# Projection units beside HGRN as eight plain products, their low parts on DVE

## The chip, the cores and the metric

The kernel runs on one core of one Trainium2 chip. The metric is the device time of one execution in microseconds (us), the median of several runs. The engines are named as the profile names them: PE (matrix products, with PEld for its weight loads), DVE (vector), ACT (activation), POOL (the general-purpose engine, called `gpsimd` in the code) and SP, whose queue issues the DMAs.

## The reference, cut to what matters

Two layers of a hybrid encoder over 1024 tokens of width 1024. Each layer is

```python
h = rms_norm(x, norm_g[l])
proj = einsum("bsd,de->bse", h, w_in[l])       # one combined input projection
# proj is split into xm, om, zm | hq, ff, fb, hi, hz | aq, ak, av, az
y_m = mLSTM(xm, om, zm)        # 4 heads
y_h = HGRN2(hq, ff, fb, hi, hz)  # 6 heads of 128, both directions
y_a = differential_attention(aq, ak, av, az)   # 4 heads
x = x + concat(y_m, y_h, y_a) @ w_out[l]
```

HGRN2 in one direction is the recurrence `S_t = diag(f_t) S_{t-1} + (1 - f_t) i_t^T`, `o_t = S_t^T q_t`, with `f = lb + (1 - lb) * sigmoid(ff)`. The kernel computes it for both directions at once by doubling: at level `lv` pairs of blocks of `2**lv` tokens are joined.

## The kernel before, in words

**The projection.** `w_in` is cut into 32 units of two blocks of 128 columns each; three of them (`xm`) are done at the start of a layer, 29 are a stream (`stream`, L471) that fills PE beside the other work. The normed input, transposed, is held as four operands B11, B12, B21, B22 (halves of the depth by halves of the tokens) of 128x512 pieces. Products are made in fp32r, with each fp32 factor split into a high part `whi` (an ACT copy, L163) and a low part `wlo` (what the copy left over, a subtraction on POOL, L164), and three matmuls (hi·hi, hi·lo, lo·hi) for each of four pieces of depth: twelve matmuls of 128x512 make one product (`steps12`). A unit (`unit`, from L208) is a 2x2 block product by Strassen's method in Winograd's form: seven products instead of eight, 84 matmuls, paid with four sums of weights (`wsum`, L171; `ws` in the trace) and with the sums of B (`Bt`, t1 to t4), which are made once a layer. The results go through SBUF tiles `p`, `u`, `c` to DRAM (`pr_d`).

**The order.** `fill(n)` takes the next n steps of the stream; one step is one matmul, and a few steps only issue splits. From the mLSTM heads until 48 steps after the last HGRN head, every PE instruction is tied to the one before it (`in_order`), so the order on PE there is the written one. On the other engines, and on PE in the stages behind HGRN, a scheduler orders the instructions when the kernel is built. The table `H_FILL` (L80) says how many steps stand ahead of each piece of a HGRN head.

**A HGRN head** (`hgrn`, from L854): load and transpose the values (`hvt`); tanh of the gates on ACT, from it the keys `ks` (L877, DVE) and the gates T (L879, ACT); `kd` and `qp` by `dtt` (a `scalar_tensor_tensor` of DVE, recorded at L121); the products `dg` on PE; then seven levels. At a level ACT copies the wanted halves of both directions of `ks` to `kt` (L908, levels 0 to 4), PE makes the scores `lv`, DVE merges them into `sd` under a mask (L894), multiplies `ks` and `qp` by the gates (L121, each direction by itself from level 1 on) and then T by itself (L121). After the levels come the transposes `kst`, the states `sb`/`sf` (chains `Sb`, `Sf` on DVE, L984 and L996), the output `ho`, its squares (`jk`, L1018), the normalisation `rstd` (L427 to L433), the scaling (L1024, ACT) and the transposes `hyT`. The loop over heads (L1037) runs the start of the next head ahead of the end of the current one, so that `rstd` stands behind the next head's `ks`, `kd` and `qp` on DVE.

While the heads run, `sums["pool"]` is set, and the weight sums are made on POOL too (L175).

## Time and profile before

| what | value |
|---|---|
| median of 3 runs | 3116.47 us (3112.49 to 3120.48) |
| the profiled execution | 3109.8 us, span 3108.1 us |
| PE busy | 2729.3 us, 88% of the span |
| DVE busy | 2057.1 us, 66% |
| ACT busy | 1374.4 us, 44% |
| POOL busy | 984.5 us, 32% |
| HGRN with the 48 steps behind it, layer 1 | 491 to 975 us of the span |
| the same, layer 2 | 2027 to 2511 us |
| mean granted PE clock | 0.951 |

A row of the grouped view gives the line, the engine, the operation, its operands by the program's names, the shape and the count, then the busy time and the mean duration of one, and then how long the engine stood idle just before these instructions and what ended most of that. A row of the timeline gives start and duration in us. A row of a tile view gives the shortest, the median and the longest duration in ns.

### The profile page before, as it was taken

Reading aid. Unit: us, or ns where it says so; the run is one execution under the profiler, and the core shown is the slowest. Engines: PE = TensorE matmul, PEld = TensorE weight load, DVE = VectorE, ACT = ScalarE, POOL = GpSimd, SP = SyncE. Lnnn points to the kernel's source line nnn. Section 1 sums busy time; section 2 is a strip of 40 time slices with the busy share of each in tenths; the row PEclk is TensorE's granted clock in tenths of the full one; section 3 lists DMA queues with packets and bytes.
Section 4 is the critical chain, followed back from the end, with each engine's and each line's share of the span. In section 5 each row is a group of like instructions: output and inputs, shape, how many; then the busy total and the mean of one; then the engine's idle time right before and its main releaser. Section 6 shows DMA issues by size and latency. Waiting matters only on the chain. (4 is left out here: it accounts for less than half of the span.)

```text
span 3108.1 us, 44781 instructions
## 1 busy us (share of the span) xinstructions
PE 2729.3 (88%) x16428; PEld 2243.4 (72%) x16428; DVE 2057.1 (66%) x3690; ACT 1374.4 (44%) x2832; POOL 984.5 (32%) x725
## 2 busy tenths in 40 slices
PE   6889999888889997998979999988888898879987
PEld 4777877666667776787858787876666676768875
DVE  7776546776773646997587644467766656489964
ACT  5334544434444435654153354543444444465533
POOL 4243224443433440010241432244443343301012
PEclk9899999998999998999998999999999999999998
DMA  3343333222224654420223343332222156542221
GB/s 108 109 133 120 123 125 109 96 89 89 89 79 156 214 170 117 159 81 29 82 75 116 117 131 133 99 113 93 99 92 89 65 196 219 183 134 90 67 71 72
DMA packets 186524, 351.98 MB, mean 113 GB/s; under 512 B 17968, under 2 KB 67632, under 8 KB 186304
## 3 DMA queue, kind: packets, MB, share of 16 engines
q1 hardware_dynamic: 186304, 349.12, 34.2%
q8 instruction: 129, 2.11, 0.3%
q14 instruction: 91, 0.75, 0.1%
HBM read 234.69 MB, written 114.36 MB: 112 GB/s over the span
## 5 line engine op out<-in xcount | busy, mean ns | idle before, releaser
L164 POOL TENSOR_TENSOR wlo<-wraw,whi 128x512 fp32r<-128x512 f32 x262 | 390.3, 1496 | 1292.0 <-ACT whi L163 1152.5
L164 POOL TENSOR_TENSOR wlo<-ws,whi 128x512 fp32r<-128x512 f32 x232 | 347.3, 1498 | 581.2 <-ACT whi L163 510.9
L109 PE MATMUL op<-whi,yb 128*128 128x512 f32 x1024 | 340.3, 401 | 0.6 <-DVE ayo L1181 0.4
L163 ACT ACTIVATE whi<-wraw 128x512 fp32r<-128x512 f32 x262 | 163.5, 627 | 319.1 <-issue 99.9
L163 ACT ACTIVATE whi<-ws 128x512 fp32r<-128x512 f32 x232 | 146.1, 630 | 328.2 <-PE ua L111 139.6
L111 PE MATMUL ua<-Bt,whi 128*128 128x512 f32 x742 | 269.5, 435 | 0.5 <-DVE c L252 0.3
L1271 DVE TENSOR_TENSOR xo<-op,xo 128x512 f32<-128x512 f32 x256 | 174.1, 687 | 88.8 <-PE op L109 88.0
L109 PEld LDWEIGHTS op<-whi,yb 128*128 128x128 f32 x1024 | 193.8, 190 | 44.8 <-DVE ayo L1181 1.2
L109 PE MATMUL ua<-Bt,whi 128*128 128x512 f32 x650 | 211.9, 406 | 13.7 <-ACT u L238 9.3
L109 PE MATMUL op<-wlo,yb 128*128 128x512 f32 x512 | 202.8, 396 | 0.0
L1205 ACT ACTIVATE e<-S,mx 128x1024 f32<-128x1024 f32 x128 | 142.1, 1112 | 101.9 <-DVE mx L1202 59.1
L111 PEld LDWEIGHTS ua<-Bt,whi 128*128 128x128 f32 x742 | 148.2, 203 | 34.7 <-issue 3.3
L121 DVE SCALAR_TENSOR_TENSOR qp<-qp,T 128x512 f32<-128x512 f32 (+1 forms) x156 | 166.9, 1106 | 3.6 <-PE lv L111 3.6
L121 DVE SCALAR_TENSOR_TENSOR ks<-ks,T 128x512 f32<-128x512 f32 (+1 forms) x156 | 151.6, 1001 | 23.1 <-ACT kt L908 13.8
L1201 DVE TENSOR_REDUCE mx<-S 128x1 f32<-128x1024 f32 x128 | 155.1, 1217 | 14.7 <-PE S L109 14.2
L111 PE MATMUL ua<-Bt,wlo 128*128 128x512 f32 x372 | 160.2, 431 | 0.0
L109 PE MATMUL po<-av,wT 128*128 128x128 f32 x1024 | 141.3, 285 | 20.4 <-ACT wT L1221 10.5
L109 PEld LDWEIGHTS po<-av,wT 128*128 128x128 f32 x1024 | 131.9, 197 | 33.3 <-ACT wT L1221 15.7
L109 PEld LDWEIGHTS ua<-Bt,whi 128*128 128x128 f32 x650 | 123.5, 193 | 44.4 <-ACT u L238 10.2
L908 ACT ACTIVATE kt<-ks 128x1024 f32<-128x1024 f32 x60 | 71.3, 1188 | 149.2 <-PE lv L111 57.9
L109 PE MATMUL S<-qkh 128*128 128x512 f32 x256 | 110.6, 432 | 23.1 <-ACT e L1205 22.9
L109 PE MATMUL ua<-Bt,wlo 128*128 128x512 f32 x324 | 129.9, 401 | 0.0
(433 smaller groups left out, 6749.2 us busy)
## 6 DMA issues: line engine op xcount, KB each, us to landing
wraw<-w_in SPq DMA_DIRECT2D x256, 256.0 KB
wraw<-yT SPq DMA_DIRECT2D x64, 256.0 KB
wraw<-w_out SPq DMA_DIRECT2D x64, 256.0 KB
xac<-xcd SPq DMA_DIRECT2D x16, 512.0 KB
W<-mu SPq DMA_DIRECT2D x32, 256.0 KB
xcd<-xc SPq DMA_DIRECT2D x12, 512.0 KB
xct<-tka SPq DMA_DIRECT2D x12, 512.0 KB
vd<-tkv SPq DMA_DIRECT2D x12, 512.0 KB
```

The lines of the kernel that those rows point to most:

```text
L109: return fn(*a, **k)
L111: seq["last"] = fn(*a, **k)
L121: nc.vector.scalar_tensor_tensor(out_, a, 1.0, b, op0=ALU.mult, op1=op)
L163: nc.scalar.activation(hi, src, AF.Copy)
L164: (lo_eng or nc.gpsimd).tensor_tensor(lo, src, hi.bitcast(F32), op=ALU.subtract)
L908: nc.scalar.activation(raw(kt, 0, [[2 * hs, nb], [hs, 2], [1, hs]]), raw(ks, 0, [[2 * hs, nb], [hs + S, 2], [1, hs]]), AF.Copy)
L1201: nc.vector.tensor_reduce(mx, ps, axis=AX.X, op=ALU.max)
L1205: nc.scalar.activation(e, ps, AF.Exp, scale=QK ** -0.5, bias=mx, accum_out=ls_)
L1271: nc.vector.tensor_tensor(xv, ps, xv, op=ALU.add)
```

## The change: what it does

While the HGRN heads run (`plain["on"]`), a unit is done by `unit_plain`: eight products, 96 matmuls, from B11, B21, B22 and t1 alone, where t1 is B12 - B11. For each of the two blocks: A1·B11 is copied out as `p` and stays in PSUM, where A2·B21 is added to it; A1·t1 and A2·B22 are summed in a second PSUM tile, to which `p` is added. There are no sums of weights. A unit splits four weights instead of seven, and the low part is a `tensor_tensor` on DVE instead of POOL. `H_FILL` has 16 more steps a head. In HGRN itself, T's scaling goes from ACT to DVE (a `tensor_scalar`), the `scalar_tensor_tensor` of `kd`, `qp` and the levels become `tensor_tensor`, and at every level one instruction multiplies both directions of `ks`, and one both of `qp`, through a three-dimensional pattern that goes to and fro between the two directions.

```diff
-H_FILL = {"hvt": 0, "ty": 32, "dg": 10, 0: 14, 1: 14, 2: 10, 3: 10, 4: 10, 5: 8, 6: 14, "kst": 10, "sb": 8, "ho": 10, "tail": 60}
+H_FILL = {"hvt": 0, "ty": 36, "dg": 12, 0: 14, 1: 14, 2: 12, 3: 12, 4: 12, 5: 10, 6: 14, "kst": 10, "sb": 8, "ho": 12, "tail": 60}
...
-    def split(src, lo_eng=None):
+    plain = {"on": False}
+
+    def split(src):
...
-        (lo_eng or nc.gpsimd).tensor_tensor(lo, src, hi.bitcast(F32), op=ALU.subtract)
+        (nc.vector if plain["on"] else nc.gpsimd).tensor_tensor(lo, src, hi.bitcast(F32), op=ALU.subtract)
...
     def wsum(o, a, b, op):
-        if sums["pool"]:
-            nc.gpsimd.tensor_tensor(o, a, b, op=op)
-        else:
-            dtt(o, a, b, op)
+        dtt(o, a, b, op)
...
+    def unit_plain(l, u, B, dst):
...
+        raws = [w_quad(l, u, q) for q in range(4)]
+        o1, o2 = split(raws[0]), split(raws[1])
+        yield
+        for xy in range(2):
+            psa = ps_pj(f"va{l}_{u}{xy}")
+            yield from steps12(psa, o1, B["11"], True, True)
+            p1 = tmp(f"p{xy}")
+            nc.scalar.activation(p1, psa, AF.Copy)
+            yield
+            psd = ps_pj(f"vd{l}_{u}{xy}")
+            yield from steps12(psd, o1, B["t1"], True, False)
+            if xy == 0:
+                n1 = split(raws[2])
+            yield
+            yield from steps12(psd, o2, B["22"], False, True)
+            c = tmp(f"c{xy}2")
+            nc.vector.tensor_tensor(c, psd, p1, op=ALU.add)
...
+            if xy == 0:
+                n2 = split(raws[3])
+            yield
+            yield from steps12(psa, o2, B["21"], False, True)
+            c = tmp(f"c{xy}1")
+            nc.scalar.activation(c, psa, AF.Copy)
...
-                yield from unit(l, U_OF[a, b], B, (dst_of(a), dst_of(b)))
+                yield from (unit_plain if plain["on"] else unit)(l, U_OF[a, b], B, (dst_of(a), dst_of(b)))
...
-                nc.scalar.activation(th, th, AF.Identity, scale=lb_a1[:, l, d, hd:hd + 1], bias=lb_a2[:, l, d, hd:hd + 1])
+                nc.vector.tensor_scalar(th, th, lb_a1[:, l, d, hd:hd + 1], lb_a2[:, l, d, hd:hd + 1],
+                                        op0=ALU.mult, op1=ALU.add)
...
-            dtt(kd, ks[:, 0], ks[:, 1], ALU.add)
-            dtt(qp[:, 0], T0[:, 0], q, ALU.mult)
-            dtt(qp[:, 1], T0[:, 1], q, ALU.mult)
+            nc.vector.tensor_tensor(kd, ks[:, 0], ks[:, 1], op=ALU.add)
+            nc.vector.tensor_tensor(qp[:, 0], T0[:, 0], q, op=ALU.mult)
+            nc.vector.tensor_tensor(qp[:, 1], T0[:, 1], q, op=ALU.mult)
...
-                for src, t_ in ((ks, (W + 1, 0)), (qp, (1, W))):
-                    if lv == 0:
-                        sv = raw(src, 0, [[2, nb], [1 + S, 2]])
-                        dtt(sv, sv, raw(T, t_[0], [[2, nb], [t_[1] - t_[0], 2]]), ALU.mult)
-                    else:
-                        for w in range(2):
-                            sv = raw(src, w * (hs + S), [[2 * hs, nb], [1, hs]])
-                            dtt(sv, sv, raw(T, t_[w], [[2, nb], [0, hs]]), ALU.mult)
+                el = [[2 * hs, nb], [hs + S, 2], [1, hs]]
+                tq = raw(T, 1, [[2, nb], [W - 1, 2], [0, hs]])
+                tk = raw(T, W + 1, [[2, nb], [-W - 1, 2], [0, hs]])
+                qv = raw(qp, 0, el)
+                kv = raw(ks, 0, el)
+                nc.vector.tensor_tensor(kv, kv, tk, op=ALU.mult)
+                nc.vector.tensor_tensor(qv, qv, tq, op=ALU.mult)
...
-                dtt(raw(base, 0, [[W // 2, 2], [1, W // 2]]), a0, a1, ALU.mult)
+                nc.vector.tensor_tensor(raw(base, 0, [[W // 2, 2], [1, W // 2]]), a0, a1, op=ALU.mult)
...
-        sums["pool"] = True
+        plain["on"] = True
...
-        sums["pool"] = False
+        plain["on"] = False
```

How the order of the instructions moves, at the three places that the prediction speaks of. Rows give line, operation, output and inputs, shape and count; in the kernel after, L985 and L986 are the products of `ks` and `qp`, L990 is T's, L927 the merge, L225 a unit's sum and L166 a low part.

DVE in the second head of layer 1, around levels 1 and 2, before:

```order
L894 COPY_PREDICATED sd_4991<-lvl_96,lv_5101 128x512
L121 SCALAR_TENSOR_TENSOR qp_4863<-qp_4863,T_10_5031 128x256x2 x2
L121 SCALAR_TENSOR_TENSOR ks_4864<-ks_4864,T_01_4862 128x128x4 x2
L121 SCALAR_TENSOR_TENSOR T_10_5031<-T_01_4862 128x256
L894 COPY_PREDICATED sd_4991<-lvl_97,lv_5143 128x512
L121 SCALAR_TENSOR_TENSOR qp_4863<-qp_4863,T_01_4862 128x128x4 x2
```

The same place now:

```order
L927 COPY_PREDICATED sd_4936<-lvl_96,lv_5054 128x512
L986 TENSOR_TENSOR qp_4827<-qp_4827,T_10_4986 128x256x2x2
L985 TENSOR_TENSOR ks_4828<-ks_4828,T_01_4826 128x128x2x4
L990 TENSOR_TENSOR T_10_4986<-T_01_4826 128x256
L166 TENSOR_TENSOR wlo_5393<-wraw_5254,whi_5392 128x512
L927 COPY_PREDICATED sd_4936<-lvl_97,lv_5093 128x512
L986 TENSOR_TENSOR qp_4827<-qp_4827,T_01_4826 128x128x2x4
```

Each pair of `ks` or `qp` products has become one instruction of twice the elements, in the same order, and a unit's low part stands between them.

DVE at the change of heads, from the end of head 1's state chain to its `rstd`, before:

```order
L996 SCALAR_TENSOR_TENSOR ks_4864<-ks_4864,Tc_5350,sf_5429 128x128 x4
L877 TENSOR_SCALAR ks_5504<-T_02_5502,nlb_a_114,lb_a_112 128x1024 x2
L121 SCALAR_TENSOR_TENSOR kd_5612<-ks_5504 128x1024
L121 SCALAR_TENSOR_TENSOR qp_5503<-T_02_5502,hq_5505 128x1024 x2
L252 TENSOR_TENSOR c_15_5574<-ua_15_5312,p_15_5555 128x512
L427 TENSOR_SCALAR rs_5525<-hss_5445 128x8
```

The same place now:

```order
L1028 SCALAR_TENSOR_TENSOR ks_4828<-ks_4828,Tc_5292,sf_5356 128x128 x4
L166 TENSOR_TENSOR wlo_5635<-wraw_5624,whi_5634 128x512
L909 TENSOR_SCALAR ks_5428<-T_02_5426,nlb_a_114,lb_a_112 128x1024 x2
L911 TENSOR_SCALAR T_02_5426<-T_02_5426,lb_a_112,lb_a_113 128x1024 x2
L914 TENSOR_TENSOR kd_5540<-ks_5428 128x1024
L225 TENSOR_TENSOR c_15_5475<-vd_150_5332,p_15_5330 128x512
L916 TENSOR_TENSOR qp_5427<-T_02_5426,hq_5429 128x1024
L915 TENSOR_TENSOR qp_5427<-T_02_5426,hq_5429 128x1024
L459 TENSOR_SCALAR rs_5449<-hss_5372 128x8
```

Two `tensor_scalar` (L911, T's scaling) have come in ahead of `kd`, and a low part ahead of `ks`.

POOL at the end of the mLSTM stage of layer 1 and into HGRN, before (`ws` is a sum of weights):

```order
L164 TENSOR_TENSOR wlo_4199<-ws_3932,whi_4198 128x512
L175 TENSOR_TENSOR ws_4375<-wraw_4269,wraw_4273 128x512
L164 TENSOR_TENSOR wlo_4236<-wraw_3842,whi_4235 128x512
L164 TENSOR_TENSOR wlo_4278<-wraw_4269,whi_4277 128x512
L164 TENSOR_TENSOR wlo_4282<-wraw_4271,whi_4281 128x512
```

The same place now, with the running numbers in the names (`wlo149` is the 149th):

```order
L166 TENSOR_TENSOR wlo148_4097<-ws147_4094,whi148_4096 128x512
L166 TENSOR_TENSOR wlo149_4199<-ws144_3932,whi149_4198 128x512
L166 TENSOR_TENSOR wlo243_7972<-wraw239_7963,whi243_7971 128x512
L166 TENSOR_TENSOR wlo244_7976<-wraw240_7965,whi244_7975 128x512
L166 TENSOR_TENSOR wlo247_8166<-ws246_8163,whi247_8165 128x512
```

POOL goes from the last low part ahead of HGRN (149) straight to the first behind it (243). On PE the order of the HGRN pieces is the same; the matmuls of units between them are 96 more in each layer's HGRN (1033 instead of 937 from the first `hvt` to the first `soT` behind HGRN), and 36 more from there to the end of the layer's stream (753 instead of 717).

More of the change, by code (lines that the diff above doesn't have):

```diff
@@ L169, in w_quad @@
         return load_raw(w_in[l, :, o:o + 512])
-    sums = {"pool": False}
     def wsum(o, a, b, op):
-        if sums["pool"]:
-            nc.gpsimd.tensor_tensor(o, a, b, op=op)
-        else:
-            dtt(o, a, b, op)
+        dtt(o, a, b, op)
     def w_tmp():
@@ L206, in unit_std, with tmp @@
                 evac(xy, ps, half)
+    def unit_plain(l, u, B, dst):
+        def tmp(nm):
+            return un.tile([P, 512], F32, tag="ut", name=f"{nm}{l}_{u}")
+        raws = [w_quad(l, u, q) for q in range(4)]
[15 more added lines that the diff above has]
+            nc.vector.tensor_tensor(c, psd, p1, op=ALU.add)
+            for rows, ap in dst[xy]:
+                nc.sync.dma_start(ap[:, 512:], c[rows])
+            if xy == 0:
[4 more added lines that the diff above has]
+            nc.scalar.activation(c, psa, AF.Copy)
+            for rows, ap in dst[xy]:
+                nc.sync.dma_start(ap[:, :512], c[rows])
+            if xy == 0:
+                o1, o2 = n1, n2
+                yield
     def unit(l, u, B, dst):
```

## The prediction

> **What bounds the kernel now.** The page comes first, for the engines' shares:
>
> ```profile
> span 3108.1 us, 44781 instructions
> PE 2729.3 (88%) x16428; PEld 2243.4 (72%) x16428; DVE 2057.1 (66%) x3690; ACT 1374.4 (44%) x2832; POOL 984.5 (32%) x725
> ```
>
> PE is the busiest, but 88% is a mean over stages. The change touches HGRN and, through what is left of the stream, the stage behind it. So the second view is the stages: HGRN with its 48 last steps in both layers, then the stage behind it.
>
> ```profile
> core 0: us, PE busy (x) PEld busy (x) DVE busy (x) ACT busy (x) POOL busy (x), PEclk, DMA share, GB/s
> 491.00:975.00 484.00, 400.56 (x3363) 322.79 (x3361) 335.55 (x505) 198.84 (x392) 207.57 (x125) 0.93 0.29 96
> 2027.00:2511.00 484.00, 404.03 (x3378) 326.14 (x3377) 333.05 (x508) 201.58 (x395) 209.28 (x125) 0.93 0.29 99
> 975.00:1160.00 185.00, 169.15 (x740) 136.14 (x741) 97.61 (x152) 79.16 (x165) 76.49 (x54) 0.95 0.61 201
> ```
>
> HGRN takes 484 us in either layer; PE is idle for 83 and 80 of them, 82 on average, and its clock is at 0.93. Third, the PE groups of 491 to 975, for the waits; the last three rows are of layer 2's stretch.
>
> ```profile
> L111 PE MATMUL lv<-qp,kt 128*64 128x64 f32 x960 | 38.1, 234 | 22.7 <-DVE qp L121 19.6 <-ACT u L238 1.9 <-ACT p L222 1.3
> L111 PE MATMUL kst<-ident,ks 128*128 128x128 f32 x96 | 14.0, 292 | 10.8 <-ACT kst L972 10.2 <-DVE ks L121 0.5
> L111 PE MATMUL hyT<-ident,ho 128*128 128x128 f32 x48 | 13.7, 454 | 24.4 <-ACT ho L1024 24.4
> L111 PE MATMUL ho<-hv,sc 128*128 128x128 f32 x96 | 12.3, 281 | 10.0 <-DVE Sb L984 10.0
> L111 PE MATMUL lv<-qp,ks 128*64 128x64 f32 x192 | 7.7, 240 | 6.6 <-DVE qp L121 6.6
> L111 PE MATMUL dg<-hq,kd 128*64 128x64 f32 x192 | 7.4, 233 | 3.0 <-DVE kd L121 3.0
> L111 PE MATMUL lv<-qp,ks 128*32 128x32 f32 x384 | 4.6, 199 | 5.0 <-DVE qp L121 5.0
> ...
> L111 PE MATMUL lv<-qp,kt 128*64 128x64 f32 x960 | 39.8, 240 | 25.7 <-DVE qp L121 25.6
> L111 PE MATMUL hyT<-ident,ho 128*128 128x128 f32 x48 | 13.7, 436 | 24.4 <-ACT ho L1024 24.4
> L111 PE MATMUL kst<-ident,ks 128*128 128x128 f32 x96 | 13.2, 281 | 3.7 <-ACT kst L972 3.7
> ```
>
> The waits end at DVE: the levels wait for `qp`, and `hyT` for ACT's scaling, which follows DVE's `rstd`. The units' own matmuls show hardly a wait. Why DVE is late, its groups and POOL's of the same stretch tell:
>
> ```profile
> L121 DVE SCALAR_TENSOR_TENSOR qp<-qp,T 128x512 f32<-128x512 f32 x72 | 68.4, 989 | 1.3 <-PE lv L111 1.3
> L121 DVE SCALAR_TENSOR_TENSOR ks<-ks,T 128x512 f32<-128x512 f32 x72 | 63.2, 909 | 4.5 <-PE lv L111 4.3
> L894 DVE COPY_PREDICATED sd<-lvl,lv 128x512 f32<-128x512 uint8 x30 | 22.1, 736 | 0.1
> L121 DVE SCALAR_TENSOR_TENSOR qp<-qp,T 128x1024 f32<-128x1024 f32 x6 | 14.9, 2485 | 0.0
> L164 POOL TENSOR_TENSOR wlo<-ws,whi 128x512 fp32r<-128x512 f32 x48 | 78.4, 1634 | 147.0 <-ACT whi L163 118.1 <-ACT jk L1018 12.3 <-PE ua L111 11.4
> ...
> L121 DVE SCALAR_TENSOR_TENSOR qp<-qp,T x156: 653/685/2694, 521.7 to 2464.9; 128x512 f32<-128x512 f32 x144, 128x1024 f32<-128x1024 f32 x12
> L121 DVE SCALAR_TENSOR_TENSOR kd<-ks x12: 1224/1226/2172, 512.1 to 2409.7; 128x1024 f32<-128x1024 f32 x12
> L410 DVE TENSOR_TENSOR kk<-kk 128x1024 f32<-128x1024 f32 x1 | 1.2, 1226 | 0.5 <-ACT kk L407 0.5
> ...
> L121 DVE SCALAR_TENSOR_TENSOR T<-T 128x512 f32<-128x512 f32 x6 | 5.2, 859 | 0.0
> ```
>
> A `qp` product of 512 elements has a median of 0.685 us and a mean of 0.99: most run undisturbed, the others take about 1.1 us more. Disturbed ones run beside a POOL subtraction or sum. The same shows in small instructions, 0.17 against 1.1 to 1.2 us within one `rstd`, below. So POOL's 125 instructions cost DVE some 70 of its 335 us here: 144 level products by 0.95 - 0.68 make 39, the rest is in T, `rstd`, `kd` and the copies.
>
> **The change, part by part, per layer.** (a) *More matmuls.* `H_FILL` rises from 150 to 166 steps a head; by six heads that is 96 matmuls. A row of the chain of waits has the price of a product at full clock:
>
> ```profile
> 2569.19 2.79 PE ub L109 x12
> ```
>
> 2.79 / 12 = 0.2325 us, so +22.3 us of PE. This is certain work; only whether it falls into waits is open, and that is counted in (b).
>
> (b) *The waits.* First the levels. POOL gone, a level's DVE work is merge 0.74, `qp` and `ks` in one instruction each, T (halved at each level; the last row above is level 1's; say 0.35 on average) and a unit's share. A `tensor_tensor` of 1024 costs 1.226 by `kk`, as a `scalar_tensor_tensor` does (`kd`). The unit's share: four low parts and two sums at 0.685, as a product of 512 takes, make 4.1 us per 97 steps, 0.5 per 12. Together 0.74 + 2.45 + 0.35 + 0.5 = 4.0 us. Before it was 0.74 + 2 x (0.99 + 0.91) + 0.5 + 0.4 = 5.4. PE has, per level, 12 matmuls (2.8) and `lv` (32 x 0.036 = 1.15, from the 38.1 us of 960 overlapping ones): 3.95 us. So DVE and PE come out even, and `ks` can be multiplied while PE runs `lv`. Left over is level 0, whose `qp` keeps its 2.5 us: I leave 1.3 us a head there and 0.7 at levels 5 and 6. The `lv` waits go from 34 (22.7 + 6.6 + 5.0) to 12.
>
> The price of the merged instructions is the unknown. Their pattern goes to and fro between the directions after 2, 4, 8... elements; level 0 does so after each, and costs 2.2 to 2.7 us for 1024. ACT's `kt` copy reads in just that pattern already, here levels 0, 1 and 2:
>
> ```profile
> 513.34 1.53 ACT L908 ACTIVATE kt<-ks 128x1024 f32<-128x1024 f32 x1
> 521.09 1.20 ACT L908 ACTIVATE kt<-ks 128x1024 f32<-128x1024 f32 x1 [1.03 <-DVE hz L1004]
> 525.74 1.06 ACT L908 ACTIVATE kt<-ks 128x1024 f32<-128x1024 f32 x1 [1.68 <-PE lv L111]
> ```
>
> 1.53, 1.20, 1.06: from runs of four on nothing is paid. I take 1.23 us from level 2 on and up to 0.3 more at level 1; the ends are 1.23 and level 0's 2.49.
>
> Then `hyT`. The change from the first head to the second, in time:
>
> ```profile
> 567.79 1.73 PE L111 MATMUL ho<-ks,qp 128*128 128x128 f32 x14
> 569.35 1.04 PE L111 MATMUL hvt<-ident,hvT 128*128 128x128 f32 x8
> 569.62 1.54 DVE L877 TENSOR_SCALAR ks<-T,nlb_a,lb_a 128x1024 f32<-128x1024 f32 x2 [6.27 <-PE ho L111]
> 577.84 1.23 DVE L427 TENSOR_SCALAR rs<-hss 128x8 f32<-128x8 f32 x1
> 579.10 1.18 DVE L428 TENSOR_SCALAR rs<-rs 128x8 int32<-128x8 int32 x1
> 583.07 0.17 DVE L433 SCALAR_TENSOR_TENSOR hr<-rs,hr 128x8 f32<-128x8 f32 x1
> 583.69 2.28 PE L111 MATMUL hyT<-ident,ho 128*128 128x128 f32 x8 [5.71 <-ACT ho L1024]
> ```
>
> From the end of `ho` (569.5) to `hyT` are 14.2 us: 8.3 until DVE has made the next head's `ks`, `kd`, `qp`, 5.4 of `rstd` with three instructions disturbed (two shown), nearly 1 us each. Now: `ks` 1.5, T's two `tensor_scalar` another 1.5 (new, and right on this path), `kd` and two `qp` 3.4, one unit sum 0.6, a low part 0.6, `rstd` 2.6, ACT 0.4: 10.6 us. PE covers `hvt` 1.0 and 36 matmuls 8.4, together 9.4. The wait is 1.2 a head instead of 4.1: 24 becomes 7. Were T's scaling hidden, nothing would be left; were `rstd` disturbed as before, 24.
>
> `ho`'s 10 us is the chain `Sb` on PSUM, untouched: 10 stays. `kst` waits for ACT to empty PSUM: 7 on average, stays. `dg` 3 stays. New: the units' matmuls now wait for low parts from DVE's queue, behind level products. In the order they stand some 60 PE instructions ahead of their use, so I take 3 us, bounds 0 and 35 (0.4 us at each of 84 products). Sum of waits: 82 becomes 12 + 7 + 10 + 7 + 3 + 3 = 42, so -40. Bounds 25 and 70.
>
> (c) *The clock.* 1 - 0.93 over 484 us is 34 us of lost clock at most. Slow stretches follow the waits, as this one:
>
> ```profile
> 657.40:664.00 6.60, 6.04 (x18) 4.52 (x18) 2.21 (x4) 2.17 (x8) 2.56 (x2) 0.50 0.45 151
> 684.39 0.88 PE L111 MATMUL lv<-qp,kt 128*64 128x64 f32 x14 [1.86 <-ACT u L238]
> 684.70:688.00 3.30, 3.30 (x33) 2.85 (x31) 3.30 (x6) 1.14 (x2) 0.68 (x1) 0.50 0.25 79
> ```
>
> The first is behind a `hyT` wait, at half clock for 6.6 us, and costs 3.3. The second follows a wait of just 1.86 us. With `hyT` at 1.2 us most of the six long stretches go (20 us), but waits of nearly 2 us still trip it: the loss goes from 34 to 16, -18; bounds 3 and 34. (The Trainium skill, "TensorE: Matmul & The Clock Gate", Part 1, lets the clock fall only after an idle window of about 3.4 us; the 1.86 us row speaks against taking that strictly. By it the loss would go to 0, and the whole forecast would be 32 us lower; the sum goes by the rows.)
>
> (d) *The stage behind.* Units done at the layer's 48-step end are fewer by 36 matmuls: the stream has 753 behind HGRN instead of 717. PE is busy 169 of 185 us there, so +8.4 us in full; bounds 0 and 8.4.
>
> (e) *At nothing:* ACT loses three splits a unit and T's scaling, and has waits of its own; if it did matter it would be a gain. DMAs are as many as before (four loads, the same stores a unit). DVE's sum: 335 - 70 + 28 (42 low parts) + 10 (T) - 7 (sums) - 9 (merging) = 287 us, below PE, so its total hides.
>
> Sum per layer: 22.3 - 40 - 18 + 8.4 = -27.3; two layers -55. The profiled execution (3109.8 us, span 3108.1) becomes 3055; it lies 6.7 us under the median of the runs, 3116.5, which becomes **3062 us**.
>
> **The rivals.**
>
> *The merged products run at level 0's rate* (the other side). Then a level costs DVE 0.74 + 2 x 2.49 + 0.35 + 0.5 = 6.6 us, 1.2 more than before; by 6 levels and 6 heads +43. `hyT` still gains 17, the clock 10; the steps outside the levels (8 a head) add 11, (d) 8.4. That is +35 a layer, 3187 us. It decides from about 1.9 us an instruction on, where a level costs what it did. For it: the 2485 row. Against it: ACT's 1.06. Chance 8%.
>
> *PE waits for DVE's low parts and sums.* At the bound of 35 us a layer instead of 3, the change gives -55 + 64 = +9: 3126 us; at 30 the gain is just used up, 3116, no change. For it: in the stage behind HGRN PE does wait for a unit's sum on DVE:
>
> ```profile
> L109 PE MATMUL ud<-Bt,whi 128*128 128x512 f32 x62 | 22.8, 453 | 7.1 <-DVE c L232 7.1
> ```
>
> Against it: a low part stands far ahead, and DVE has 287 us of work in a stage of 450. Chance 15%, centred on 3116.
>
> *The waits nearly all go,* to 25 us, and the clock's loss to 3: 22.3 - 57 - 31 + 8.4 = -57 a layer, 3002 us. For it: DVE and PE are even per level and I left slack. Against it: `ho`, `kst` and `dg` are 20 by themselves. Chance 15%.
>
> That POOL is not freed is excluded by the order, which has nothing on it within HGRN.
>
> **How the numbers follow.** The forecast has 62%, its own range 3035 to 3092. The range for 8 in 10 leaves out the merged-rate case, half of the large gain and the far end of the second rival: 3005 to 3121. About 0.3% (9 us) is what a measurement of this kernel can tell from no change. Faster: 61 of the forecast's 62, all 15 of the large gain, 4 of the second rival, 80%. Same: 1 + 7, 8%. Slower: 4 + 8, 12%.
>
> **What would show it.** Right: HGRN at some 448 us, plus or minus 12; `qp` and `ks` at 1.2 us; `hyT` waits of about 7 us a layer; clock 0.96 or more. Wrong: merged products above 1.9 us; PE waiting on `wlo` or `c` for over 15 us a layer; a `hyT` wait of 15 or more, which would say that `rstd`'s place in the queue and not POOL made it; or a stage behind HGRN that grows by more than 10 us.

## The result and the profile after

| kernel | us, median of the runs (from, to) | ratio to before, 95% interval |
|---|---|---|
| before | 3114.71 (3112.49 to 3120.48) | 1 |
| changed | 3000.73 (2997.70 to 3006.52) | 0.9634 [0.9612, 0.9655] |

The change gains 114 us, twice the 55 us that were forecast; 3000.73 lies 4 us below the predicted range of 3005 to 3121. The profiled execution took 2998.28 us, 111.5 less than that of before. First its page, then its stages (HGRN with the 48 steps behind it in layer 1, the stage behind, layer 1's attention and output, and HGRN and the stage behind in layer 2; the columns are those of the stages in the prediction, and the cuts are the first instruction behind the last `num` product, the first `soT` and the first `S`):

```profile
span 2996.6 us, 44714 instructions
PE 2747.8 (92%) x16692; PEld 2258.2 (75%) x16692; DVE 1978.3 (66%) x3638; ACT 1315.2 (44%) x2742; POOL 579.2 (19%) x481
...
495.18:922.43 427.25, 398.77 (x3447) 322.41 (x3445) 287.15 (x469) 166.15 (x340) 6.42 (x5) 0.99 0.32 110
922.43:1110.26 187.83, 179.59 (x801) 144.53 (x802) 104.93 (x157) 84.01 (x175) 84.13 (x58) 0.98 0.60 198
1110.26:1509.91 399.65, 363.33 (x1914) 301.34 (x1912) 307.68 (x603) 192.23 (x388) 50.38 (x37) 0.97 0.33 103
1966.46:2395.71 429.25, 400.39 (x3447) 323.70 (x3445) 287.10 (x469) 166.11 (x340) 6.42 (x5) 0.99 0.32 109
2395.71:2581.80 186.09, 178.46 (x801) 143.08 (x802) 104.59 (x157) 84.16 (x175) 85.86 (x58) 0.99 0.60 200
```

The same cuts in the kernel before:

```profile
493.11:976.72 483.61, 398.45 (x3351) 320.77 (x3350) 334.13 (x499) 198.57 (x390) 206.86 (x125) 0.93 0.29 98
976.72:1165.83 189.11, 174.98 (x765) 140.85 (x766) 101.10 (x155) 81.64 (x169) 78.71 (x55) 0.95 0.59 194
1165.83:1572.05 406.22, 365.71 (x1914) 304.02 (x1912) 306.32 (x604) 191.87 (x389) 50.17 (x37) 0.95 0.32 101
2029.30:2508.90 479.60, 399.63 (x3351) 322.05 (x3350) 330.16 (x499) 198.28 (x390) 208.20 (x125) 0.93 0.29 99
2508.90:2693.83 184.93, 171.10 (x765) 137.94 (x766) 101.22 (x155) 81.71 (x169) 77.77 (x55) 0.98 0.59 198
```

HGRN is 56.4 and 50.4 us shorter, together 106.7 of the 111.5. The stage behind it is as long as before (-1.3 and +1.2) though it holds 36 more matmuls. Layer 1's attention is 6.6 shorter; nothing of the change is in it, and other kernels below whose work there is that of before take 399 to 406 us for it, so this is counted as chance. In HGRN PE was idle for 85.2 and 80.0 us (length less busy time) and is now for 28.5 and 28.9. Its busy time is unchanged, although 96 matmuls were added: the clock gave their 22 us back. DVE stands at 287 us, the figure that was forecast.

What is left of PE's waits in layer 1's HGRN, and then DVE's groups of the same stretch:

```profile
L111 PE MATMUL lv<-qp,kt 128*64 128x64 f32 x960 | 37.3, 231 | 5.1 <-DVE qp L986 4.9 <-ACT kt L941 0.2
L111 PE MATMUL kst<-ident,ks 128*128 128x128 f32 x96 | 13.1, 279 | 1.5 <-ACT kst L1004 1.5
L111 PE MATMUL ho<-hv,sc 128*128 128x128 f32 x96 | 12.3, 281 | 10.0 <-DVE Sb L1016 10.0
L111 PE MATMUL hyT<-ident,ho 128*128 128x128 f32 x48 | 11.9, 333 | 5.2 <-ACT ho L1056 5.2
L111 PE MATMUL dg<-hq,kd 128*64 128x64 f32 x192 | 6.9, 225 | 2.0 <-DVE kd L914 2.0
L111 PE MATMUL va<-B,whi 128*128 128x512 f32 x352 | 116.1, 406 | 1.0 <-ACT c L233 1.0
```

```profile
L985 DVE TENSOR_TENSOR ks<-ks,T 128x1024 f32<-128x1024 f32 x42 | 57.0, 1358 | 6.7 <-ACT kt L941 6.2 <-PE lv L111 0.4
L986 DVE TENSOR_TENSOR qp<-qp,T 128x1024 f32<-128x1024 f32 x42 | 56.9, 1355 | 2.2 <-PE lv L111 2.0
L166 DVE TENSOR_TENSOR wlo<-wraw,whi 128x512 fp32r<-128x512 f32 x42 | 28.7, 684 | 18.7 <-ACT whi L165 17.6 <-PE va L111 1.0
L927 DVE COPY_PREDICATED sd<-lvl,lv 128x512 f32<-128x512 uint8 x30 | 22.2, 741 | 6.6 <-PE lv L111 6.4
L909 DVE TENSOR_SCALAR ks<-T,nlb_a,lb_a 128x1024 f32<-128x1024 f32 x12 | 9.3, 810 | 21.5 <-PE ho L111 11.6 <-PE hvt L111 5.4 <-ACT T L908 4.5
...
L986 DVE TENSOR_TENSOR qp<-qp,T x84: 1190/1217/2237, 523.4 to 2354.6; 128x1024 f32<-128x1024 f32 x84
```

`hyT` fell from 24.4 to 5.2 us, `lv` from 22.7 (and 6.6 and 5.0 at the last levels) to 5.1 and next to nothing, `kst` from 10.8 to 1.5. `ho`, which nothing touched, is the largest wait now. The merged products have a median of 1.22 us; only level 0 takes 2.2 us, which lifts the mean to 1.36. No product waits for a low part.

### The profile page after: what moved, and what is told of

Its sections match the earlier page's. It is cut to its first block, busy times and chain, and to the rows that moved or that the text cites. A ratio compares the mean times of both kernels' runs of the same rounds, so it can differ in the third digit from the quotient of the medians.

```text
span 2996.6 us, 44714 instructions
## 1 busy us (share of the span) xinstructions
PE 2747.8 (92%) x16692; PEld 2258.2 (75%) x16692; DVE 1978.3 (66%) x3638; ACT 1315.2 (44%) x2742; POOL 579.2 (19%) x481
## 5 line engine op out<-in xcount | busy, mean ns | idle before, releaser
L166 POOL TENSOR_TENSOR wlo<-wraw,whi 128x512 fp32r<-128x512 f32 x194 | 279.9, 1450 | 1845.2 <-ACT whi L165 1686.2
L166 POOL TENSOR_TENSOR wlo<-ws,whi 128x512 fp32r<-128x512 f32 x144 | 199.6, 1388 | 348.9 <-ACT whi L165 338.2
L111 PE MATMUL va<-B,whi 128*128 128x512 f32 x704 | 232.9, 407 | 1.9 <-ACT c L233 1.9
L109 PE MATMUL ua<-Bt,whi 128*128 128x512 f32 x666 | 214.1, 402 | 8.3 <-DVE c L284 7.7
L111 PEld LDWEIGHTS va<-B,whi 128*128 128x128 f32 x704 | 133.1, 193 | 33.4 <-ACT c L233 2.8
L109 PEld LDWEIGHTS ua<-Bt,whi 128*128 128x128 f32 x666 | 123.6, 190 | 38.7 <-DVE c L284 10.8
L111 PE MATMUL va<-B,wlo 128*128 128x512 f32 x352 | 143.7, 408 | 0.0
L109 PE MATMUL ua<-Bt,wlo 128*128 128x512 f32 x332 | 132.4, 399 | 0.0
L121 DVE SCALAR_TENSOR_TENSOR ws<-wraw,wraw 128x512 f32<-128x512 f32 x72 | 60.8, 844 | 100.0 <-POOL wlo L166 36.9
L985 DVE TENSOR_TENSOR ks<-ks,T 128x1024 f32<-128x1024 f32 x84 | 114.0, 1358 | 13.4 <-ACT kt L941 12.4
```

Of the source, the lines that this page charges most:

```text
L109: return fn(*a, **k)
L111: seq["last"] = fn(*a, **k)
L121: nc.vector.scalar_tensor_tensor(out_, a, 1.0, b, op0=ALU.mult, op1=op)
L166: (nc.vector if plain["on"] else nc.gpsimd).tensor_tensor(lo, src, hi.bitcast(F32), op=ALU.subtract)
L985: nc.vector.tensor_tensor(kv, kv, tk, op=ALU.mult)
```

## The experiments

Three explanations of the gain were put against each other. **A:** POOL's instructions beside DVE made DVE late, and PE's waits and clock followed; so the gain is POOL's silence. **B:** the work itself got less (no sums of weights, half the low parts, merged products), wherever it is done. **C:** the 16 additional steps a head stand where PE waited. The table has all kernels; each ratio is to runs of the kernel before that were made beside it (medians of 3109 to 3115 us); HGRN is the length of the stage in layers 1 and 2 of the profiled execution, and DVE and POOL are DVE's busy time and POOL's instructions in it, in layer 1.

| kernel | us, median (from, to) | ratio to before, 95% interval | HGRN us | DVE us | POOL x |
|---|---|---|---|---|---|
| before | 3114.71 (3112.49 to 3120.48) | 1 | 484, 480 | 334 | 125 |
| changed | 3000.73 (2997.70 to 3006.52) | 0.9634 [0.9612, 0.9655] | 427, 429 | 287 | 5 |
| low parts on POOL | 3026.76 (3015.13 to 3033.38) | 0.9714 [0.9683, 0.9745] | 436, 436 | 284 | 48 |
| seven products, all on DVE | 3030.96 (3024.44 to 3042.93) | 0.9734 [0.9709, 0.9759] | 467, 467 | 349 | 7 |
| before, merged levels | 3087.18 (3082.27 to 3090.77) | 0.9909 [0.9892, 0.9926] | 471, 472 | 325 | 125 |
| levels apart | 2997.66 (2995.37 to 2999.18) | 0.9622 [0.9608, 0.9637] | 429, 430 | 292 | 5 |
| steps as before | 3050.77 (3047.83 to 3056.49) | 0.9803 [0.9774, 0.9832] | 416, 418 | 282 | 5 |
| steps ahead of `ho` | 2991.15 (2982.73 to 2999.18) | 0.9606 [0.9580, 0.9631] | 422, 419 | 287 | 5 |
| fewer ahead of `hyT` | 3037.70 (3033.74 to 3045.50) | 0.9764 [0.9738, 0.9789] | 448, 444 | 288 | 5 |
| 135 unread subtractions on POOL | 3134.47 (3133.11 to 3134.51) | 1.0071 [1.0047, 1.0094] | 492, 487 | 355 | 140 |
| 45 unread subtractions on POOL | 3023.03 (3019.52 to 3029.67) | 0.9701 [0.9679, 0.9724] | 438, 438 | 306 | 50 |
| POOL writes only | 3023.71 (3019.62 to 3027.31) | 0.9701 [0.9680, 0.9722] | 440, 436 | 293 | 306 |
| T on ACT | 3009.96 (3001.53 to 3020.64) | 0.9659 [0.9629, 0.9689] | 429, 427 | 280 | 5 |
| no low part on POOL anywhere | 2954.05 (2951.05 to 2964.55) | 0.9482 [0.9457, 0.9506] | 419, 419 | 290 | 0 |

### POOL's work alone, put back

```diff
-        (nc.vector if plain["on"] else nc.gpsimd).tensor_tensor(lo, src, hi.bitcast(F32), op=ALU.subtract)
+        (nc.vector if plain["on"] else nc.gpsimd).tensor_tensor(lo, src, hi.bitcast(F32), op=ALU.subtract)
+        if plain["on"]:
+            for i in range(3):
+                dmy = plain["gp"].tile([P, 512], F32R, tag="dmy", name=f"dmy{cnt['n']}_{i}", bufs=1)
+                nc.gpsimd.tensor_tensor(dmy, hi.bitcast(F32), hi.bitcast(F32), op=ALU.subtract)
```

> The changed kernel with work added on POOL alone: with each of the 45 splits a layer beside HGRN POOL makes three subtractions of 128x512 of the split's high part from itself into a tile that nothing reads, 135 a layer, about as many as POOL had before (125). PE, DVE and ACT do what they do in the changed kernel; the output stays as it was. Theory A (POOL's traffic disturbs DVE, and PE's waits and clock follow): the level products' mean goes from 1.36 back to about 1.7 us, DVE's sum from 287 to some 345 us, waits of the levels and of hyT return, +40 to +65 us a layer: 3080 to 3130 us, nearly all of the gain. Theory B (what counts is how much work DVE was relieved of, and POOL beside it costs little, as the run with only the low parts back on POOL suggests, +8 us a layer in HGRN): 3001 to 3030 us.

3134.47 us: all 114 us of the gain are gone, and 20 more. DVE's and POOL's groups, PE's waits, and the whole stage, in layer 1:

```profile
L990 DVE TENSOR_TENSOR ks<-ks,T 128x1024 f32<-128x1024 f32 x42 | 71.1, 1693 | 8.0 <-ACT kt L946 7.9
L991 DVE TENSOR_TENSOR qp<-qp,T 128x1024 f32<-128x1024 f32 x42 | 65.4, 1557 | 0.8 <-PE lv L111 0.8
L166 DVE TENSOR_TENSOR wlo<-wraw,whi 128x512 fp32r<-128x512 f32 x42 | 40.7, 970 | 21.9 <-ACT whi L165 20.8 <-PE va L111 1.0
L932 DVE COPY_PREDICATED sd<-lvl,lv 128x512 f32<-128x512 uint8 x30 | 21.9, 731 | 3.0 <-PE lv L111 3.0
L229 DVE TENSOR_TENSOR c<-vd,p 128x512 f32<-128x512 f32 x22 | 15.0, 681 | 4.8 <-PE vd L111 3.1 <-DMA T<-pr_fb 1.7
L914 DVE TENSOR_SCALAR ks<-T,nlb_a,lb_a 128x1024 f32<-128x1024 f32 x12 | 12.1, 1045 | 20.0 <-PE ho L111 11.2 <-PE hvt L111 5.4 <-ACT T L913 3.4
L170 POOL TENSOR_TENSOR dmy<-whi 128x512 fp32r<-128x512 f32 x135 | 226.4, 1677 | 251.2 <-ACT whi L165 207.0 <-DMA hsd<-hsum 36.1
...
L111 PE MATMUL lv<-qp,kt 128*64 128x64 f32 x960 | 39.2, 238 | 21.4 <-DVE qp L991 20.7 <-ACT c L237 0.6
L111 PE MATMUL kst<-ident,ks 128*128 128x128 f32 x96 | 13.7, 288 | 4.3 <-ACT kst L1009 3.5 <-DVE ks L990 0.8
L111 PE MATMUL hyT<-ident,ho 128*128 128x128 f32 x48 | 12.5, 415 | 20.8 <-ACT ho L1061 20.8
...
493.52:985.20 491.68, 416.50 (x3448) 335.77 (x3446) 355.19 (x469) 165.69 (x340) 232.76 (x140) 0.94 0.29 95
```

DVE makes the same 469 instructions as in the changed kernel and takes 355.2 us for them instead of 287.2: 68 us of disturbance, where the prediction had read 70 out of the trace of before. The waits of `lv` and `hyT` come back to about 21 us each, the clock to 0.94, and HGRN grows by 64 and 58 us. Nothing else was changed, so theory A is shown as a cause that is large enough by itself. The way is not through the high parts, which POOL now holds longer: ACT waits for POOL only 6.5 us in layer 1, and the units' products (`va`) 2.2 us instead of 1.0.

The rows also say which instructions of DVE are held up. `ks`, `qp`, the low parts and the `TENSOR_SCALAR`s, whose data are all in SBUF, take 0.1 to 0.34 us more on average; the mask copy (0.731 against 0.741) and the unit's sum `c` (0.681 against 0.687), which read a PSUM tile, take no longer. The shortest, median and longest duration show it for single instructions (`sd<-lvl,lv` reads PSUM, the copy `sc<-sd` only SBUF):

```profile
L932 DVE COPY_PREDICATED sd<-lvl,lv x60: 708/733/758, 527.0 to 2476.9; 128x512 f32<-128x512 uint8 x60
L983 DVE COPY sc<-sd x24: 408/424/1272, 555.1 to 2481.9; 64x512 f32<-64x512 f32 x24
```

(The Trainium skill, "SBUF — State Buffer", "Who interferes with whom", says that a DVE instruction with two SBUF inputs contends with a GpSimd instruction that reads SBUF, and one with at most one does not unless it is in a two-port mode, which a copy and `tensor_scalar` can enter; these rows agree.)

### The same with POOL work that reads nothing, and with a third of it

```diff
+        if plain["on"]:
+            for i in range(7):
+                nc.gpsimd.memset(src, 0.0)
```

> The changed kernel with POOL work that reads nothing: after each of the 45 splits a layer beside HGRN POOL fills the weight tile that has just been read with zeros, seven times, some 0.55 us each by the 0.42 of a fill of 128x386, so about 173 us of POOL a layer, as the 135 subtractions take undisturbed. The output stays as it was; the weight buffers come free some 4 us later. If any POOL instruction holds DVE up: as with the subtractions, 3090 to 3135 us, level products at a mean of 1.6 us. If only POOL's reads of SBUF do: level products at 1.36 us, 3001 to 3020 us (more only if the weight loads come late, which would show as waits for the weights).

```profile
L988 DVE TENSOR_TENSOR ks<-ks,T 128x1024 f32<-128x1024 f32 x42 | 57.0, 1358 | 11.9 <-ACT kt L944 11.5 <-PE lv L111 0.4
L989 DVE TENSOR_TENSOR qp<-qp,T 128x1024 f32<-128x1024 f32 x42 | 56.9, 1354 | 2.2 <-PE lv L111 2.0
L912 DVE TENSOR_SCALAR ks<-T,nlb_a,lb_a 128x1024 f32<-128x1024 f32 x12 | 10.6, 920 | 21.6 <-PE ho L111 16.3 <-ACT T L911 5.3
L169 POOL MEMSET wraw<- 128x512 f32 x301 | 161.5, 540 | 247.0 <-DVE wlo L166 233.2
```

POOL is busy for 162 us with it, and the level products are exactly as in the changed kernel, 1358 and 1354 ns. The `TENSOR_SCALAR`s are still held up, 920 against 810. So it is what POOL reads that delays the products with two SBUF inputs; its writes are enough to delay the other kind. (The same section of the Trainium skill, "SBUF — State Buffer", has it so.) The time was 3023.71 us, 23 above the changed kernel and a little above the second number; DVE's sum grew by only 6 us, and `lv` also waits 2.5 us for ACT's `kt`. Whether the rest is the weight tiles that come free later was not tried.

With `range(1)` in place of `range(3)` in the diff of the unread subtractions:

> A third of the additional POOL work of the run with three unread subtractions at each split (+134 us): one at each split, 45 a layer, PE, DVE and ACT as in the changed kernel. If the price is per POOL subtraction that meets DVE: +45 us, 3045 us. If slack on DVE takes the first part in (the run with only the low parts back on POOL, 48 subtractions a layer and 29 us less on DVE, came to +26): +20 us or less, 3010 to 3020 us.

3023.03 us, +22, and 9.4 us a layer in HGRN for 19 us more on DVE: a third of the traffic costs a sixth of the 134 us, a little above the second number. That fits slack on DVE which takes in the first part; after it each us on DVE is nearly a us of time (50 more on DVE, 52 more in HGRN, from this run to the one with 135).

### Low parts back on POOL; seven products on DVE

```diff
-        (nc.vector if plain["on"] else nc.gpsimd).tensor_tensor(lo, src, hi.bitcast(F32), op=ALU.subtract)
+        nc.gpsimd.tensor_tensor(lo, src, hi.bitcast(F32), op=ALU.subtract)
```

> The changed kernel with one thing undone: the 42 low parts a layer that belong to HGRN's units are made on POOL again, not on DVE. Eight products, the merged level products and the table of steps stay, so PE does the same work. Theory A (POOL's traffic beside DVE is what made DVE late, and PE's waits and clock followed): 42 of before's 125 POOL instructions are back, so about a third of the disturbance (70 us of DVE a layer) returns, some 25 us, and a third of the 85 us of waits and lost clock: about +28 us a layer, 3055 us; the level products show again a mean above their median. Theory B (the shorter DVE work of the merged products is what counted): DVE is relieved of 28 us a layer of low parts, the time is 2990 to 3002 us. Theory C (the additional steps ahead of the waits did it): nothing changes, 3001 us within 0.3%.

3026.76 us: between the theories, at half of what A said. The stages show 8 and 7 us of it in HGRN; the rest is spread over stages that were not touched. A's number left out that DVE is rid of 29 us of low parts: DVE's sum is 284 us with the disturbance, 287 without it. By itself, where HGRN's low parts are made is worth 26 of the 114 us.

```diff
-                yield from (unit_plain if plain["on"] else unit)(l, U_OF[a, b], B, (dst_of(a), dst_of(b)))
+                yield from unit(l, U_OF[a, b], B, (dst_of(a), dst_of(b)))
```

> The changed kernel, but the units beside HGRN are the seven-product ones of before, with their low parts, sums of weights and sums of products all on DVE; nothing is on POOL there. The table of steps stays, so PE does as many steps in HGRN, and some 124 matmuls a layer less behind it. DVE gets some 75 us a layer more than the changed kernel (287 to 362). Theory A (POOL's disturbance, not DVE's load): DVE stays below PE's 400 us; a level's DVE work grows from 4.0 to about 5.3 us against PE's 3.95, so some 45 us a layer of waits at the levels and 10 of clock, less 29 of the matmuls: about +25 a layer, 3050 us, with undisturbed DVE instructions (mean at the median). Theory A': DVE's slack of 140 us takes it in, the clock stays: 3001 - 58 = 2943 us. Theory B (DVE's load as such made it late, no matter whether POOL or DVE): with the load of before (335 us) passed, the waits and the clock of before come back: about +85 - 29 a layer, 3110 us.

3030.96 us. HGRN is 39 us a layer longer than in the changed kernel, and the stage behind some 18 shorter (131 fewer matmuls by the trace). `lv`, `hyT` and DVE in layer 1:

```profile
L111 PE MATMUL lv<-qp,kt 128*64 128x64 f32 x960 | 37.2, 231 | 10.1 <-DVE qp L986 9.9
L111 PE MATMUL hyT<-ident,ho 128*128 128x128 f32 x48 | 13.7, 438 | 22.1 <-ACT ho L1056 22.1
...
L985 DVE TENSOR_TENSOR ks<-ks,T 128x1024 f32<-128x1024 f32 x42 | 57.1, 1360 | 8.2 <-ACT kt L941 8.1
L166 DVE TENSOR_TENSOR wlo<-ws,whi 128x512 fp32r<-128x512 f32 x48 | 33.0, 687 | 4.9 <-ACT whi L165 4.8
...
497.86:964.84 466.98, 409.86 (x3446) 329.32 (x3445) 348.91 (x572) 193.85 (x391) 8.98 (x7) 0.96 0.32 106
```

Not one instruction is disturbed (1.360, 0.687), and yet `hyT` waits 22 us, as before: 349 us of work on DVE delay `rstd` as 355 us with disturbance do. So A alone is not the explanation either: DVE's plain load counts too. But a us of disturbance costs more than a us of work. `lv` waits 10 us here and 21 in the run with 135 unread subtractions; PE is idle for 57 us of this stage, for 75 in that run, and for 85 and 80 in the kernel before, where DVE's sum is only 334 and 330 (though 96 matmuls fewer cover its waits). And with the low parts back on POOL DVE's sum is 3 us below that of the changed kernel, and HGRN still 8 us longer. Why a us of disturbance costs more was not tried. By the times, seven products with POOL silent, the merged levels and the new steps keep some 84 of the 114 us; the eight products, which leave DVE less side work, buy the other 30 on balance.

### Merging the levels, apart and by itself; T on ACT

The first run takes the merged products out of the changed kernel, the second puts them into the kernel before:

```diff
-                nc.vector.tensor_tensor(kv, kv, tk, op=ALU.mult)
-                nc.vector.tensor_tensor(qv, qv, tq, op=ALU.mult)
+                for src, t_ in ((ks, (W + 1, 0)), (qp, (1, W))):
+                    ...
+                        for w in range(2):
+                            sv = raw(src, w * (hs + S), [[2 * hs, nb], [1, hs]])
+                            dtt(sv, sv, raw(T, t_[w], [[2, nb], [0, hs]]), ALU.mult)
```

> The changed kernel with one thing undone: the level products of ks and qp are done per direction again, four scalar_tensor_tensor of 512 a level in place of two tensor_tensor of 1024. Theory A (POOL): undisturbed they take 0.65 us each, so DVE gets 9 us a layer more and the levels wait for qp some 5 to 10 us a layer more: 3010 to 3020 us. Theory B (merging counted): half or more of the 114 us is gone, 3055 us or more.

> The kernel before with one part of the change alone: the level products of both directions of ks and of qp merged into one instruction each. Seven products, low parts and sums on POOL, and the table of steps stay as before. Theory A (POOL): a merged product is disturbed as the two apart were, since POOL's 125 instructions a layer take as long; only the fixed cost of 72 instructions a layer goes (9 us of DVE): -8 to -15 us a layer, 3085 to 3100 us. Theory B (merging is what counted): half or more of the change's 114 us, 3055 us or less.

Without POOL the merging is worth nothing (2997.66 us; the intervals of the ratios overlap), with POOL 27 us, of which 10 a layer stand in HGRN. DVE's `qp` rows of the two, in layer 1:

```profile
L121 DVE SCALAR_TENSOR_TENSOR qp<-qp,T 128x512 f32<-128x512 f32 x72 | 46.2, 685 | 1.1 <-PE lv L111 1.1
```

```profile
L953 DVE TENSOR_TENSOR qp<-qp,T 128x1024 f32<-128x1024 f32 x42 | 71.7, 1707 | 1.5 <-PE lv L111 1.5
```

Undisturbed, two products of 0.685 cost 1.37 and a merged one 1.22. Disturbed, the two apart cost 1.98 (0.989 each, in the prediction) and a merged one 1.57 from level 1 on; the 1.71 of the row holds level 0's 2.5 us too. In a layer the 156 products apart lose some 40 us to POOL and the 84 merged ones 27: fewer instructions catch fewer delays, though each catches more. A's number held for the second run (3085 to 3100); for the first it was 12 us too high (3010 to 3020), since `lv` waits only 2 us a layer more. B's fell in both.

```diff
-                nc.vector.tensor_scalar(th, th, lb_a1[:, l, d, hd:hd + 1], lb_a2[:, l, d, hd:hd + 1],
-                                        op0=ALU.mult, op1=ALU.add)
+                nc.scalar.activation(th, th, AF.Identity, scale=lb_a1[:, l, d, hd:hd + 1], bias=lb_a2[:, l, d, hd:hd + 1])
```

> The changed kernel with one thing undone: T's scaling (12 instructions a layer of 0.81 us on DVE) is on ACT again. DVE gets 9.3 us a layer less, and 1.6 us a head of it lie on the way from ho to hyT; ACT has 262 us of slack in a stage of 428 us. If DVE's order before rstd is what hyT waits for (5 us a layer are left of that wait): -5 us a layer, 2990 us. If ACT's copies for kst and kt then come late: the kst wait goes back towards 7 us and the time to 3005 to 3015 us.

3009.96 us with an interval that overlaps that of the changed kernel; HGRN has the same length. `hyT`'s wait fell by 1 us and `lv`'s rose by 3; `kst` stayed at 1.5, so the second number was met without its reason. Moving T made no difference that these runs can tell.

### Where the steps stand

```diff
-H_FILL = {"hvt": 0, "ty": 36, "dg": 12, 0: 14, 1: 14, 2: 12, 3: 12, 4: 12, 5: 10, 6: 14, "kst": 10, "sb": 8, "ho": 12, "tail": 60}
+H_FILL = {"hvt": 0, "ty": 32, "dg": 10, 0: 14, 1: 14, 2: 10, 3: 10, 4: 10, 5: 8, 6: 14, "kst": 10, "sb": 8, "ho": 10, "tail": 60}
```

> The changed kernel with the table of steps of before: 150 steps a head instead of 166, so 96 matmuls a layer move from HGRN into the stage behind it; nothing else changes. What the runs so far say: PE is without a wait in the stage behind (801 matmuls by 0.2325 us make 186.2 of its 186 to 188 us), so they cost 22.3 us a layer there; in HGRN they are 22.3 us less, of which the waits take some back (4 of the 16 stand ahead of hyT, 2 ahead of dg, 8 at levels 2 to 5 where DVE is about even with PE): 10 to 20 us a layer. Theory A (the waits went because DVE is no longer late): 3020 to 3045 us. Theory C (the additional steps ahead of the waits made the gain): half of the 114 us or more is gone, 3055 us or more. If the stage behind still had room: 2960 to 2990 us.

```profile
500.78:916.57 415.79, 382.75 (x3352) 308.27 (x3350) 281.60 (x462) 160.51 (x332) 6.64 (x5) 0.98 0.32 108
916.57:1137.38 220.81, 202.46 (x884) 161.54 (x885) 108.72 (x164) 90.47 (x185) 92.23 (x65) 0.97 0.55 178
```

3050.77 us, 50 above the changed kernel and a little above A's range. HGRN got only 11.5 us a layer shorter, so 96 matmuls worth 22.3 cost half of that there. The stage behind got 33 and 37 us longer. It has 83 matmuls more, not 96 (one unit fewer is done with eight products), worth 19 us; the other 14 to 17 are for the most part PE's idle time, 18 and 20 us there instead of 8, as PE waits again for sums of DVE and ACT. So the steps are worth 50 of the 114 us, nearly the half that C asked for, once DVE is in time for them. The new table in the kernel before was not run; in the kernel with 135 unread subtractions they stand in the same places, and HGRN is longer than before.

The next two move steps within a head:

```diff
-... "sb": 8, "ho": 12, ...
+... "sb": 8, "hs": 8, "ho": 4, ...
...
+            gap("hs")
             zt = slab(f"hzt{hd}", "q")
```

> The changed kernel with 8 of the 12 steps that stand between the two halves of the output ho moved ahead of its first half, where PE waits 1.67 us a head for the chain Sb to free its PSUM tile; nothing else changes. If that wait is simply uncovered time, 10 us a layer go, and the waits after it do not grow since the chain Sf is done 2.4 us after Sb: 2981 us. If Sf (or the square and rstd behind ho) is what the second half or hyT then waits for, the 10 us come back there: 3001 us.

2991.15 us. The wait of `ho` fell from 10.0 us to 0.8, and none of the others grew by more than 2. HGRN is 5.3 and 10.7 us shorter. The runs spread over 16 us, and the intervals of the ratios still touch; the stage shows the gain more surely than the time.

```diff
-... "ty": 36, ... "ho": 12, ...
+... "ty": 24, ... "ho": 24, ...
```

> The changed kernel with 12 of the 36 steps that stand ahead of hyT moved ahead of the second half of ho: the same work, but each hyT wait grows by 12 x 0.2325 = 2.8 us, from about 1 to about 4 us, as it was in the kernel before. It measures what such a wait costs with its clock. If a wait costs only its own time: 16.7 us a layer, 3034 us, clock as in the changed kernel. If the clock falls behind each such wait as it did before (some 6.8 us at half rate, 3.4 lost): 20 us a layer more, 3075 us, mean clock 0.955.

```profile
L111 PE MATMUL hyT<-ident,ho 128*128 128x128 f32 x48 | 13.6, 426 | 19.5 <-ACT ho L1056 19.5
...
493.32:941.27 447.95, 406.44 (x3448) 328.99 (x3446) 287.68 (x468) 165.62 (x340) 6.17 (x5) 0.97 0.32 105
```

3037.70 us: the wait costs its own time (14.3 us a layer) and 4 to 8 us of clock, read from PE's busy time, 406.4 and 404.4 instead of 398.8 and 400.4. Each of these `hyT` waits is about 3.2 us long, so the price of clock is near 1 us a wait and not the 3.4 that the second number had assumed.

### A version that beats both

The steps ahead of `ho`, and the low parts on DVE in every stage:

```diff
-        (nc.vector if plain["on"] else nc.gpsimd).tensor_tensor(lo, src, hi.bitcast(F32), op=ALU.subtract)
+        nc.vector.tensor_tensor(lo, src, hi.bitcast(F32), op=ALU.subtract)
```

> A version that may beat both kernels: the changed kernel with the 8 steps ahead of the first half of ho (2991 us), and the low parts of the units on DVE in all stages, not only beside HGRN; POOL keeps only what is no split. In the other stages POOL makes some 338 subtractions in all, DVE stands at 54 to 77% there, and PE waits for DVE's sums (3.8 and 3.0 us a layer in the stage behind HGRN). If POOL's traffic costs there as it does beside HGRN: 2960 to 2980 us. If DVE's additional 0.68 us for each weighs as much as the disturbance that goes, as with the 42 low parts of HGRN: 2985 to 3000 us. If the low parts queue behind DVE's long instructions and PE waits for them: above 3000 us.

```profile
PE 2732.3 (92%) x16692; PEld 2248.3 (76%) x16692; DVE 2065.6 (70%) x3976; ACT 1314.9 (44%) x2742; POOL 101.3 (3%) x143
```

2954.05 us, 47 below the changed kernel and below the lowest of the three numbers. DVE takes on 338 instructions, and its sum grows by 87 us, a quarter of a us for each instead of 0.68. The rest comes back as disturbance that is gone: the instructions that both kernels have take 119 us less, summed one by one (the `ws` of two raw weights, for one, 0.69 us on average instead of 0.84). So the reading of this case holds outside HGRN too. How the 47 us divide between the two edits was not measured side by side; the run with the first edit alone lay some 9 us below the changed kernel.

## Why the prediction was off

The direction and the chain of causes held; what failed are the sizes of three terms of the sum, (b), (c) and (d), all off to the same side. HGRN came to 427 and 429 us, below the 448 plus or minus 12 that was named as a sign of being right.

- **(a) 96 matmuls, +22.3 us a layer:** held. 3447 against 3351 are in the stage. The sum has them as a cost alone; that the changed kernel would be 50 us slower with the table of before, it did not say.
- **(b) the waits, -40: mis-sized, -54.** PE's idle time went from 82.6 to 28.7 us on average. The waits named in the forecast sum to 25 instead of 42; some 3 us more lie in smaller groups that it had not counted. Of the difference 6.5 are `lv` (12 left by the forecast, 5.5 in the trace): DVE and PE do come out even, a level starts every 4.1 us (4.0 forecast), but of the 2.0 us a head that were left at levels 0, 5 and 6 only 0.9 were needed. PE's side also had a slip: 38.1 us by 960 are 0.040 us for one `lv` and not 0.036, so PE's level takes 4.07 us and not 3.95, and covers DVE's 4.04. 5.5 are `kst`, which was said to stay at 7 since it "waits for ACT to empty PSUM": it fell to 1.5. ACT's copy itself waited for DVE, and the trace of before shows it:

```profile
L972 ACT ACTIVATE kst<-kst 128x512 f32<-128x512 f32 x24 | 13.1, 595 | 16.8 <-DVE qp L121 14.6 <-PE kst L111 2.3
```

In the changed kernel this copy waits 8.1 us, 8.0 of them for PE's own transposes; with 135 unread subtractions on POOL and ACT's work unchanged PE waits 4.3 and 7.1 us again. 2 are `hyT` (7 forecast, 5 measured), 1 is `dg` (3 and 2), and 2 are the new waits (3 forecast, 1 measured).

- **(c) the clock, -18: mis-sized, -22.** PE's busy time with 96 matmuls more is that of before, +0.3 and +0.8 us. Short waits trip the clock less often than the one row of 1.86 us had made it look; more on this below.
- **(d) the stage behind, +8.4: failed, 0.** Its lower bound was right. PE's idle time there went from 14 to 8 us, which took in 6 of the 8.4 us of the 36 matmuls; PE's busy time grew by 4.6 and 7.4 us only. That is not room that more work can count on: 83 matmuls more than the changed kernel has, and the idle time is 18 to 20 (33 to 37 us longer); 131 fewer, and it is 16 to 17. It depends on how the units' sums meet DVE's other work there; what sets it was not tried.
- **(e) at nothing:** held, as far as tried. DVE's sum was forecast to the us (287); that is partly luck, since on these cuts it started from 334 and 330 and not from 335. T makes no difference on either engine.

Per layer that is 22.3 - 54 - 22 = -53.7 in place of 22.3 - 40 - 18 + 8.4 = -27.3. Of the 57 us between the forecast 3055 and the profiled 2998, 28 are (b), 8 are (c), 17 are (d), and 4 are the other stages, which nothing changed (layer 1's attention 6.6 shorter, the rest some 2 longer).

**The rivals.** "The waits nearly all go" is what happened: 25 us of waits (25.2 in the rows above) and a clock loss of 3 (3.5 and 5.1 us by the granted clock, 32 and 34 before), 3002 us forecast. That its time comes within 4 us of the profiled one is partly luck: PE's busy time got 22 us from the clock and not 31, and the 8.4 of (d), which it had too, were 0. It had 15%, because `ho`, `kst` and `dg` were held to be 20 us by themselves; they are 13.5. The merged products at level 0's rate are out: from level 1 on they take 1.19 to 1.24 us. PE waiting for low parts is out as well: 1 us a layer, and that for ACT.

**What the argument left out.** It took DVE's freed time to be worth what single waits show. The chain is closer coupled: in the run with the unread subtractions 68 us of DVE were 64 us of HGRN in layer 1 (71 and 58 in layer 2), and with seven products on DVE 62 us of plain work were 39. The range's lower end had left out half of the one rival that then came true.

## What to carry to other kernels

Before an engine is taken for slack, see whether its instructions lengthen those of another: compare minimum and mean of one form, in the stage, and multiply by the count. Work moved off POOL pays here where it disappears, and pays even where it costs DVE 0.68 us each; but what it makes DVE do still counts, so algebra that saves matmuls and costs vector work can lose to the plain product. When a common cause goes, forecast all waits behind it together, also those that name another engine as the releaser.
